# A hybrid attention block: a fourth split buffer, and q and k of three head groups transposed on TensorE

## The chip, the cores and the metric

The kernel runs on one core of a Trainium2 chip. The metric is device time in microseconds, the median of several executions. Engines are named as in the profile: PE is TensorE (PEld its weight loads), DVE is VectorE, ACT is ScalarE, POOL is GpSimd, SP is SyncE, which only issues transfers here.

## The reference

One transformer layer over 2048 tokens of width 1024, in float32:

```python
u = rms_norm(h, norm1_w)
dq, dk, dv, sq, sk, sv = split(u @ w_in)              # 512 columns each
# differential attention: 4 heads, two softmax maps each (QK norm, T5 bias, chunk-causal mask)
attn = softmax(q0 @ k0.T + bias) - lam * softmax(q1 @ k1.T + bias);  y_A = attn @ v
# stick-breaking attention: 8 heads of 64, strictly causal
z = q @ k.T / 8
rem = reverse exclusive cumsum over keys of log_sigmoid(-z)
y_B = exp(log_sigmoid(z) + rem) @ v
h = h + concat(norm(y_A), norm(y_B)) @ w_out
u2 = rms_norm(h, norm2_w)
h = h + (silu(u2 @ w_gate) * (u2 @ w_up)) @ w_down     # 2816 hidden columns
```

## The kernel before

float32 factors are split into two float16 parts, hi and lo, and every product is made of three float16 products. The work has eight head groups. Groups 0 to 3 hold one differential head each (two maps), groups 4 to 7 two stick-breaking heads each. After attention come the output projection, which starts beside the last group's attention, and the feed-forward, which does not use any of the code that the change touches.

**Projection of a group.** `proj` goes over 16 tiles of 128 tokens. `proj_tile` makes 24 matmuls of 384 columns into a PSUM tile `pj`. The pool `psj` has two of these. `proj_out` copies v, and for groups 4 to 7 q and k, out of PSUM as hi and lo parts (`split_psum`: the hi part on ScalarE or VectorE, the lo part on VectorE). q and k go into the tile `st`, of which there are two. After every fourth tile `proj_batch` makes the transposed operands of the scores: `kT` and the upper half of `qT` by DMA transposes from `st` (L381), and the lower half of `qT`, which holds the same with hi and lo halves of the partitions swapped, by two copies within SBUF (L383). All of them are issued by SyncE. A group has four batches. `st` is allocated with six blocks of columns; q uses blocks 0 and 1, k blocks 2 and 3. The output projection later takes tiles of the same tag for its residual rows (L763).

**Stick-breaking attention of a group.** A unit is one block of 128 queries, one head (m) and up to 1024 keys (b). `stage_a` does a unit: score matmuls into `sc` (L457, four PSUM buffers), two sigmoids on ScalarE (L563, L566), a product scan on VectorE (L568), a multiplication on VectorE or GpSimd (L569), and then `split_t`: the hi part by a cast on ScalarE (L89, by way of `to16`), the lo part by a subtraction on GpSimd (L98, by way of `tt`), both into a tile `s16`, of which there are SB, and a DMA transpose of it into one of five tiles `aT` (L412). `stage_b` multiplies `aT` with v on TensorE (L467). Five units lie between the two (PD).

**Order.** Each engine and SyncE's queue work in order. The order is made by the framework's planner from the program's order, priorities and its own estimate of durations. Projections of group g+1 are spread over the attention of group g by `advance`. Where a step may run on several engines, `pick` takes the engine with the lowest tally of estimated work.

The buffer counts and the split of probabilities:

```python
QB, KB, ZB, AB, SB, PD = 4, 7, 9, 5, 3, 5
s16 = s16p.tile([P, 2048], F16, tag="s16", bufs=SB, name=nm("s16"))
to16(s16[:, :n], src, n, he)
tt(s16[:, n : 2 * n], src, s16[:, :n], ALU.subtract, n, le)
SP.dma_start_transpose(aT[:, : 2 * n // P, :], s16[:, : 2 * n])
```

Of the kernel before, what the change touches and what calls it, by code (L numbers as in the profile page):

```python
# [11 lines left out]
F32 = mybir.dt.float32  # L12
F16 = mybir.dt.float16
# [8 lines left out]
S, D, P = 2048, 1024, 128  # L22
# [13 lines left out]
KW = {"A": 1.0, "D": 1.0, "P": 1.0}  # L36
AHEAD = 2
AHN = 0
QB, KB, ZB, AB, SB, PD = 4, 7, 9, 5, 3, 5
XL = (0, 4, 5, 2, 1, 6, 3)  # L40
CU = 3
WE = "AP"
# [17 lines left out]
def block(tc, a, out):  # L60
    nc = tc.nc
    PE, ACT, DVE, POOL, SP = nc.tensor, nc.scalar, nc.vector, nc.gpsimd, nc.sync
    top = ExitStack()
    with top:
# [8 lines left out]
        def note(e, ns):  # L73
            load[e] += ns * KW[e]

        def pick(**cost):
            e = min(cost, key=lambda k: load[k] + cost[k] * KW[k])
            load[e] += cost[e] * KW[e]
            return e
# [5 lines left out]
        def to16(dst, src, n, engines="ADP", psum=False):  # L85
            cost = {"A": 0.84 * n + 110, "D": (1.05 if psum else 0.53) * n + 70, "P": 1.1 * n + 80}
            e = pick(**{k: cost[k] for k in engines})
            if e == "A":
                ACT.copy(dst, src)  # L89
            elif e == "D":  # L90
                DVE.tensor_copy(dst, src)
            else:
                POOL.tensor_scalar(dst, src, 1.0, 0.0, op0=ALU.mult, op1=ALU.add)

        def tt(dst, a_, b_, op, n, engines="DP"):
            cost = {"D": 1.15 * n + 70, "P": 2.45 * n + 80}
            e = pick(**{k: cost[k] for k in engines})
            (DVE if e == "D" else POOL).tensor_tensor(dst, a_, b_, op)  # L98

        def pri(k):  # L100
            def deco(f):
                @functools.wraps(f)
                def g(*args):
                    with tc.high_priority(PRI[k]) if PRI[k] else nullcontext():
                        return f(*args)
                return g
            return deco

        def nm(s):
            uid[0] += 1  # L110
            return f"{s}{uid[0]}"
# [7 lines left out]
        id16 = cp.tile([P, P], F16, name="id16")  # L119
# [25 lines left out]
        def rstd(dst, ss, mul, eps):  # L145
            n = dst.shape[-1]
            if n > 1:
                ACT.activation(dst, ss, AF.Identity, bias=eps, scale=mul)
            else:
                DVE.tensor_scalar(dst, ss, mul, eps, op0=ALU.mult, op1=ALU.add)  # L150
            POOL.tensor_tensor(dst, dst, mhalf[:, :n], ALU.pow)
# [104 lines left out]
        psj = top.enter_context(tc.tile_pool(name="psj", bufs=2, space=PSUM, side="right"))  # L256
        pjs = ExitStack()
        pp = pjs.enter_context(tc.tile_pool(name="pp", bufs=2, side="right"))

        with ExitStack() as ph1:  # L260
# [95 lines left out]
            @pri("pb")  # L356
            def proj_batch(g, G, B):
                st, v, raw = B
                qT = sp.tile([P, 4, 4, P], F16, tag="qT", bufs=QB, name=nm("qT"))
                kT = sp.tile([P, 2, 4, P], F16, tag="kT", bufs=KB, name=nm("kT"))  # L360
                if g < 4:
                    rq = raw[:].rearrange("p t (c e) -> p t c e", e=64)
                    sq = st[:].rearrange("p c t s e -> p (c t s e)")[:, :2048].bitcast(F32)
                    ACT.activation(sq.rearrange("p (t c e) -> p t c e", t=4, c=4), rq, AF.Square)
                    note("A", 950)
                    ss = sm.tile([P, 16], F32, tag="ss", bufs=2, name=nm("ss"))
                    DVE.tensor_reduce(ss[:], sq.rearrange("p (c e) -> p c e", e=64), op=ALU.add, axis=AX.X)
                    rs = sm.tile([P, 16], F32, tag="rs", bufs=2, name=nm("rs"))
                    rstd(rs[:], ss[:], 2.0 ** -16 / 64, G["epsk"][:])
                    rsb = rs[:].rearrange("p (t c) -> p t c", c=4).unsqueeze(3).to_broadcast([P, 4, 4, 64])  # L370
                    DVE.tensor_tensor(rq, rq, rsb, ALU.mult)
                    note("D", 2300)
                    gb = gk[:].unsqueeze(1).unsqueeze(1).to_broadcast([P, 4, 2, 64])
                    tt(rq[:, :, 2:4, :], rq[:, :, 2:4, :], gb, ALU.mult, 512)
                    for o in range(2):
                        src = rq[:, :, 2 * o : 2 * o + 2, :]
                        d = st[:, 2 * o : 2 * o + 2].rearrange("p c t s e -> p t c s e")
                        to16(d[:, :, :, 0, :], src, 512)
                        tt(d[:, :, :, 1, :], src, d[:, :, :, 0, :], ALU.subtract, 512)
                for T, c in ((qT[:, 2:4], 0), (kT[:], 2)):  # L380
                    SP.dma_start_transpose(T.rearrange("p c t n -> p (c t) n"), st[:, c : c + 2].rearrange("p c t s e -> p (c t s e)"))  # L381
                for o in (0, 64):
                    SP.dma_start(qT[o : o + 64, 0:2].rearrange("p c t n -> p (c t n)"), qT[64 - o : 128 - o, 2:4].rearrange("p c t n -> p (c t n)"))  # L383
                G["q"].append(qT)
                G["k"].append(kT)
                G["v"].append(v)

            def proj(g, G, fresh=None):
                for t in range(NT):
                    if fresh is not None:  # L390
                        feed(t)
                        xt = ahead.pop(0)
                    else:
                        xt = pp.tile([P, 2 * D], F16, tag="xt", bufs=3, name=nm("xt"))
                        SP.dma_start(xt[:], xs[t])
                    if t % 4 == 0:
                        st = pp.tile([P, 6, 4, 2, 64], F16, tag="st", name=nm("st"))
                        v = sp.tile([P, 4, 256], F16, tag="v", bufs=KB, name=nm("v"))
                        raw = pp.tile([P, 4, 256], F32, tag="raw", name=nm("raw")) if g < 4 else None
                    pj = proj_tile(G, xt)  # L400
                    proj_out(g, G, pj, (st, v, raw), t % 4)
                    if t % 4 == 3:
                        proj_batch(g, G, (st, v, raw))
                    yield
# [223 lines left out]
            def feed(t):  # L628
                while nx[0] < min(NT, t + AHEAD + AHN):
                    nq.append(fresh(nx[0]))  # L630
                    nx[0] += 1
                while nx[1] < min(NT, t + AHEAD):
                    ahead.append(fresh_t(*nq.pop(0)))
                    nx[1] += 1
# [120 lines left out]
            def out_proj():  # L755
                for t in range(NT):
                    mt = pp.tile([P, 2 * D], F16, tag="xt", bufs=3, name=nm("mt"))[:].rearrange("p (k n) -> p k n", k=KT)
                    with tc.high_priority(PRI["wm"]) if PRI["wm"] else nullcontext():
                        mts.append(SP.dma_start(mt, ms[t]))
                    if t in spare:  # L760
                        xf = spare[t].bitcast(F32)
                    else:
                        xf = pp.tile([P, 6, 4, 2, 64], F16, tag="st", name=nm("xf"))[:].rearrange("p c t s e -> p (c t s e)").bitcast(F32)[:, :D]  # L763
                    SP.dma_start(xf, x[t * P : (t + 1) * P, :])
                    for h in range(2):
                        po = psj.tile([P, 512], F32, tag="pj", name=nm("po"))
                        for n in range(2):
                            q = 0
                            sl = slice(256 * n, 256 * n + 256)
                            for kt in range(KT):  # L770
                                for xi, wi in ((0, 0), (0, 1), (1, 0)):
                                    PE.matmul(po[:, sl], lhsT=mt[:, kt, P * xi : P * xi + P], rhs=wos[2 * h + n][wi][:, kt, :], start=q == 0, stop=q == 23)  # L772
                                    q += 1
                            xl = xf[:, 512 * h + 256 * n : 512 * h + 256 * n + 256]
                            DVE.scalar_tensor_tensor(xl, po[:, sl], kos[2 * h + n][:], xl, op0=ALU.mult, op1=ALU.add)  # L775
                    note("D", 1400)
                    SP.dma_start(hd[t], xf)
                    if t >= 12:
                        yield
                        continue  # L780
                    post(t, xf)
                    yield
# [459 lines left out]
```

## Time and profile before

| | |
|---|---|
| median of 3 executions | 2723.46 us (2717.96 to 2725.68) |
| the profiled execution | 2726.11 us, span 2724.3 us |
| granted TensorE clock, mean | 0.975 |
| busy: PE, DVE, ACT, POOL | 2471.4, 1945.7, 1345.8, 1569.3 us |
| HBM read and written | 265.27 MB, 151.52 MB |

Busy time is an average over stages. By the start times of the lines, groups 0 to 3 end near 600 us, groups 4 to 6 run to about 1120 us, group 7 with the output projection to about 1450 us, and the feed-forward from there to the end. In the profile, a row such as "ACT s L89 <- DMA aT<-s: 79.6, 57, 3.6" says that ScalarE stood idle before its instruction of line 89 that writes tile s, until a DMA of aT<-s landed: 79.6 us in total, 57 times, 3.6 us at most. "SPq" is the queue of SyncE; the time of a transfer there is the time its issue held the queue, and "to landing" runs from the start of the issue.

### The profile page before, as it was taken

The numbers are of one execution on the slowest core, as the hardware profiler recorded it, in microseconds if no ns is written. First come the engines' busy times: TensorE is split into PE (matmuls) and PEld (weight loads), VectorE is DVE, ScalarE is ACT, GpSimd is POOL, SyncE is SP. The second block draws the span as 40 slices with busy tenths as digits, with TensorE's granted clock in tenths as the row PEclk, the third lists the DMA queues.
The fourth block names the chain that finished last, engine by engine and source line by source line (L and its number), as shares of the span: only waits on it lengthen the run. The fifth ranks groups of instructions, "written<-read, shape, count | busy, mean of one in ns | idle before, by whom it ended". The sixth has DMA issues, their size and how long they took to land. (4 is left out here: it accounts for less than half of the span.)

```text
span 2724.3 us, 45559 instructions
## 1 busy us (share of the span) xinstructions
PE 2471.4 (91%) x17084; PEld 1404.6 (52%) x17084; DVE 1945.7 (71%) x3716; ACT 1345.8 (49%) x2483; POOL 1569.3 (58%) x1134
## 2 busy tenths in 40 slices
PE   7998989898888786779888999999999999999998
PEld 4655655555555453557775444444444444444443
DVE  6898979698888988876666877777786544444445
ACT  4665656567878878765644535444352112111121
POOL 2577767667767777765655666575674232323223
PEclk9999999999999997999999999999999999999999
DMA  6788797779999998996797675666749744545534
GB/s 223 205 168 176 149 195 161 177 170 206 208 207 203 205 183 159 205 202 199 203 268 266 237 245 201 220 215 212 251 170 350 279 175 145 224 151 190 208 125 166
DMA packets 649134, 551.92 MB, mean 203 GB/s; under 512 B 506624, under 2 KB 574208, under 8 KB 638672
## 3 DMA queue, kind: packets, MB, share of 16 engines
q1 hardware_dynamic: 647088, 546.92, 73.2%
q8 instruction: 134, 2.20, 0.3%
q0 software_dynamic: 512, 1.36, 0.2%
q10 hardware_dynamic: 1312, 0.72, 0.1%
q14 instruction: 88, 0.72, 0.1%
HBM read 265.27 MB, written 151.52 MB: 153 GB/s over the span
## 5 line engine op out<-in xcount | busy, mean ns | idle before, releaser
L329 PE MATMUL pj<-w,xt 128*128 128x384 f16 x3072 | 570.1, 333 | 26.3 <-DVE st L339 10.8
L98 POOL TENSOR_TENSOR s<-z,s 128x1024 f16<-128x1024 f32 (+7 forms) x288 | 477.5, 1667 | 99.3 <-ACT s L89 94.8
L329 PEld LDWEIGHTS <-xt 128*128 128x128 f16 x3072 | 298.5, 100 | 233.8 <-issue 38.2
L568 DVE TENSOR_TENSOR_SCAN z<-z,sc 128x512 f32<-128x512 f32 (+3 forms) x320 | 352.9, 1112 | 81.4 <-ACT sc L566 39.3
L1048 PE MATMUL pd<-wd,act 128*128 128x512 f16 x1848 | 405.3, 379 | 3.9 <-DVE hs L1054 2.4
L457 PE MATMUL sc<-kT,qT 128*128 128x512 f16 (+3 forms) x1280 | 339.6, 357 | 51.7 <-DVE z L568 16.2
L467 PE MATMUL yp<-v,aT 128*128 128x64 f16 (+1 forms) x4896 | 279.6, 207 | 91.5 <-DMA aT<-s 90.4
L467 PEld LDWEIGHTS <-aT 128*128 128x128 f16 x4896 | 242.2, 101 | 181.9 <-DMA aT<-s 120.2
L98 POOL TENSOR_TENSOR act<-cg,act 128x512 f16<-128x512 f32 x117 | 166.3, 1434 | 239.4 <-ACT act L1006 133.1
L950 PEld LDWEIGHTS <-wg 128*128 128x128 f16 x1848 | 181.1, 98 | 222.0 <-issue 7.9
L1048 PEld LDWEIGHTS <-act 128*128 128x128 f16 x1848 | 180.6, 98 | 222.7 <-issue 4.8
L950 PEld LDWEIGHTS <-wu 128*128 128x128 f16 x1848 | 181.9, 99 | 219.0 <-issue 6.5
L98 POOL TENSOR_TENSOR hs<-hs,cu 128x512 f32<-128x512 f32 x132 | 166.9, 1269 | 220.9 <-DVE hs L1054 76.0
L98 POOL TENSOR_TENSOR fst<-fst 128x512 f32<-128x512 f32 x97 | 182.6, 1883 | 161.3 <-DVE wd L224 89.9
L1054 DVE SCALAR_TENSOR_TENSOR hs<-pd,c,hs 128x512 f32<-128x512 f32 x192 | 141.6, 748 | 155.6 <-PE pd L1048 151.9
L89 ACT CAST s<-z 128x384 f16<-128x384 f32 (+7 forms) x216 | 171.6, 800 | 133.5 <-DMA aT<-s 104.5
L563 ACT ACTIVATE z<-sc,c 128x512 f32<-128x512 f32 (+3 forms) x320 | 207.0, 650 | 25.7 <-PE sc L457 18.5
L569 POOL TENSOR_TENSOR z<-z,z 128x512 f32<-128x512 f32 (+3 forms) x148 | 151.5, 1027 | 100.7 <-DVE z L568 85.6
L772 PE MATMUL po<-wo,mt 128*128 128x256 f16 x1536 | 180.1, 276 | 20.2 <-DVE xf L775 11.2
L1006 ACT CAST act<-cg 128x512 f16<-128x512 f32 x132 | 81.1, 616 | 218.1 <-DVE cg L1012 173.6
L950 PE MATMUL pm<-X,wg 128*128 128x512 f16 x792 | 179.7, 380 | 0.0
L950 PE MATMUL pm<-X,wu 128*128 128x512 f16 x792 | 179.4, 379 | 0.0
(237 smaller groups left out, 4139.3 us busy)
## 6 DMA issues: line engine op xcount, KB each, us to landing
xt<-xs SPq DMA_DIRECT2D x112, 512.0 KB, 4.2
hs<-hd SPq DMA_DIRECT2D x96, 512.0 KB, 4.4
hd<-hs SPq DMA_DIRECT2D x80, 512.0 KB, 4.4
split<-wg SPq DMA_DIRECT2D x11, 1792.0 KB, 11.3
split<-wu SPq DMA_DIRECT2D x11, 1792.0 KB, 10.4
split<-wd SPq DMA_DIRECT2D x11, 1792.0 KB, 10.5
wg<-split SPq DMA_DIRECT2D x11, 1792.0 KB, 7.2
wd<-split SPq DMA_DIRECT2D x11, 1792.0 KB, 8.9
```

The source lines that it names most:

```text
L89: ACT.copy(dst, src)
L98: (DVE if e == "D" else POOL).tensor_tensor(dst, a_, b_, op)
L329: PE.matmul(pj[:, :384], lhsT=xv[:, xi, kt, :], rhs=G["w"][:, wi, kt, :], start=n == 0, stop=n == 23)
L457: PE.matmul(sc[:, : 128 * w].rearrange("p (t n) -> p t n", n=P), lhsT=G["q"][i // 4][:, 2 - 2 * o + m, i % 4, :], rhs=G["k"][q][:, m, 0:w, ...
L467: PE.matmul(yp[:, y0 : y0 + wd], lhsT=aT[:, a_, :], rhs=v[:, v_ : v_ + wd], start=start and j == 0 and q == 0, stop=stop and j == nb - 1 a ...
L563: ACT.activation(om[:, lo:hi], sc[:, :w], AF.Sigmoid, scale=G["nkz"][:])
L568: DVE.tensor_tensor_scan(ov, ov, sc[:, :w], om[:, hi : hi + 1], op0=ALU.mult, op1=ALU.bypass)
L569: (DVE if e == "D" else POOL).tensor_tensor(be[:, lo:hi], beta, om[:, lo + 1 : hi + 1], ALU.mult)
L772: PE.matmul(po[:, sl], lhsT=mt[:, kt, P * xi : P * xi + P], rhs=wos[2 * h + n][wi][:, kt, :], start=q == 0, stop=q == 23)
L950: PE.matmul(ps_[:].rearrange("p (t n) -> p t n", n=P), lhsT=wv[:, wo, wi, 128 * kt : 128 * kt + 128], rhs=X[xo][:, :, xi, kt, :], start=st ...
L1048: PE.matmul(po[:], lhsT=act[:, ao, xi, 128 * j : 128 * j + 128], rhs=W["d"][:, wo, wi, :], start=start and u == 0 and q == 0, stop=u == nu ...
L1054: DVE.scalar_tensor_tensor(dst, po[:], kd[:], src, op0=ALU.mult, op1=ALU.add)
```

## The change

The count SB goes from 3 to 4. For groups 5, 6 and 7 `proj_batch` makes `kT` and both halves of `qT` on TensorE: eight transposes of 128x128 for k, eight for q, and sixteen of 64 columns for the swapped q, into three PSUM tiles of the pool `psj` read as 1024 float16. Each tile is copied to SBUF by ScalarE or VectorE (`to16` with the engines "AD"). Groups 0 to 4 keep the DMA transposes and copies. The tile `st` has four blocks in place of six.

```diff
-QB, KB, ZB, AB, SB, PD = 4, 7, 9, 5, 3, 5
+QB, KB, ZB, AB, SB, PD = 4, 7, 9, 5, 4, 5
...
-                for T, c in ((qT[:, 2:4], 0), (kT[:], 2)):
-                    SP.dma_start_transpose(T.rearrange("p c t n -> p (c t) n"), st[:, c : c + 2].rearrange("p c t s e -> p (c t s e)"))
-                for o in (0, 64):
-                    SP.dma_start(qT[o : o + 64, 0:2].rearrange("p c t n -> p (c t n)"), qT[64 - o : 128 - o, 2:4].rearrange("p c t n -> p (c t n)"))
+                if g > 4:
+                    for T, c, sw in ((kT[:], 2, 0), (qT[:, 2:4], 0, 0), (qT[:, 0:2], 0, 1)):
+                        pt = psj.tile([P, 512], F32, tag="pj", name=nm("qkt"))[:].bitcast(F16)
+                        for b in range(8):
+                            blk = st[:, c + b // 4, b % 4]
+                            if sw:
+                                for o in range(2):
+                                    PE.transpose(pt[64 * o : 64 * o + 64, P * b : P * b + P], blk[:, 1 - o, :], id16[:])
+                            else:
+                                PE.transpose(pt[:, P * b : P * b + P], blk.rearrange("p s e -> p (s e)"), id16[:])
+                        to16(T.rearrange("p c t n -> p (c t n)"), pt, 1024, "AD", True)
+                else:
...
-                        st = pp.tile([P, 6, 4, 2, 64], F16, tag="st", name=nm("st"))
+                        st = pp.tile([P, 4, 4, 2, 64], F16, tag="st", name=nm("st"))
...
-                        xf = pp.tile([P, 6, 4, 2, 64], F16, tag="st", name=nm("xf"))[:].rearrange("p c t s e -> p (c t s e)").bitcast(F32)[:, :D]
+                        xf = pp.tile([P, 4, 4, 2, 64], F16, tag="st", name=nm("xf"))[:].rearrange("p c t s e -> p (c t s e)").bitcast(F32)[:, :D]
```

More of the change, by code (lines that the diff above doesn't have):

```diff
@@ L379, in proj_batch @@
                         tt(d[:, :, :, 1, :], src, d[:, :, :, 0, :], ALU.subtract, 512)
-                for T, c in ((qT[:, 2:4], 0), (kT[:], 2)):
-                    SP.dma_start_transpose(T.rearrange("p c t n -> p (c t) n"), st[:, c : c + 2].rearrange("p c t s e -> p (c t s e)"))
-                for o in (0, 64):
-                    SP.dma_start(qT[o : o + 64, 0:2].rearrange("p c t n -> p (c t n)"), qT[64 - o : 128 - o, 2:4].rearrange("p c t n -> p (c t n)"))
+                if g > 4:
[10 more added lines that the diff above has]
+                else:
+                    for T, c in ((qT[:, 2:4], 0), (kT[:], 2)):
+                        SP.dma_start_transpose(T.rearrange("p c t n -> p (c t) n"), st[:, c : c + 2].rearrange("p c t s e -> p (c t s e)"))
+                    for o in (0, 64):
+                        SP.dma_start(qT[o : o + 64, 0:2].rearrange("p c t n -> p (c t n)"), qT[64 - o : 128 - o, 2:4].rearrange("p c t n -> p (c t n)"))
                 G["q"].append(qT)
```

## The prediction

> **What bounds the kernel now.** I read the page first, then the busy times by stage, then the waits of the slowest stage, then the queue of SyncE and single stretches of the timeline.
>
> ```profile
> span 2724.3 us, 45559 instructions
> core 0: us, PE busy (x) PEld busy (x) DVE busy (x) ACT busy (x) POOL busy (x), PEclk, DMA share, GB/s
> 120.00:600.00 480.00, 431.86 (x3442) 276.60 (x3440) 408.18 (x1217) 288.39 (x750) 337.93 (x240) 0.98 0.80 169
> 600.00:1210.00 610.00, 500.82 (x5177) 321.75 (x5176) 512.59 (x974) 477.68 (x887) 450.17 (x337) 0.94 1.00 198
> 1210.00:1450.00 240.00, 204.57 (x2131) 175.04 (x2129) 153.63 (x226) 122.22 (x191) 140.23 (x95) 0.97 0.82 238
> 1450.00:2724.00 1274.00, 1237.03 (x5789) 569.83 (x5786) 784.19 (x1091) 396.81 (x522) 592.22 (x407) 0.99 0.58 209
> 900.00:950.00 50.00, 38.05 (x420) 23.91 (x416) 45.34 (x64) 40.38 (x68) 40.06 (x26) 0.93 1.07 217
> ```
>
> The four long rows are differential attention, stick-breaking attention with the projections of the groups ahead, its end beside the output projection, and the feed-forward. The last is TensorE's (97% busy), and no line of the change runs in it. In 600 to 1210 no engine is full: VectorE 84%, TensorE 82%, ScalarE 78%, GpSimd 74%. The chain of waits on the page holds only the end of the feed-forward and says nothing here, so I go by the waits of this stage. Columns: who waited for whom, us in total, times, longest.
>
> ```profile
> ACT s L89 <- DMA aT<-s: 79.6, 57, 3.6
> POOL s L98 <- ACT s L89: 74.8, 58, 5.0
> PE yp L467 <- DMA aT<-s: 51.8, 45, 3.7
> DVE z L568 <- ACT sc L566: 34.3, 34, 2.3
> DVE z L568 <- ACT z L566: 30.8, 25, 3.9
> PE pj L329 <- DVE st L339: 9.1, 9, 1.8
> SPq L412 <- PE yp L467: 1.2, 1, 1.2
> ```
>
> ScalarE's cast L89 opens a split buffer (tag s16, three of them). It waits 57 times because the transfer that empties the buffer of three units ago has not landed. While it waits, the sigmoids behind it on ScalarE's queue are late, and VectorE's scan waits for these (34.3 + 30.8 us); GpSimd's subtraction waits too. The rate of a buffer follows from three rows of the same stage:
>
> ```profile
> L89 ACT CAST s<-z 128x1024 f16<-128x1024 f32 (+5 forms) x171 | 135.9, 801 | 84.0 <-DMA aT<-s 79.6 <-issue 1.7 <-POOL z L569 0.9
> L98 POOL TENSOR_TENSOR s<-z,s 128x1024 f16<-128x1024 f32 (+7 forms) x175 | 280.0, 1609 | 75.9 <-ACT s L89 74.8 <-POOL s L98 0.7
> L412 SPq DMA_TRANSPOSE aT<-s x175: 1167/1782/6477, 599.9 to 1209.0; - x175
> DMA to landing us min/median/max: 2.3/4.5/9.2
> ```
>
> A unit keeps its buffer for the cast (0.80), the subtraction (1.61) and 4.5 us from issue to landing: 6.9 us, plus waiting in the queues of GpSimd and SyncE. 171 units in 610 us are one each 3.57 us, so a slot comes round in 3 x 3.57 = 10.7 us. Only 3.8 us of a turn are left for the two queues, which is why the buffer runs out so often. By engine, a unit costs VectorE 512.6/171 = 3.00 us and ScalarE 2.79. So the three buffers, and behind them VectorE, set this stage.
>
> **The change part by part.** *Fourth buffer (SB).* It takes away ScalarE's 79.6 us of waits wherever the transfer is at most one unit late. The longest is 3.6 us, about one unit (3.57), so I expect nearly all to go. The shrunk st pays for it: two buffers of 6 x 4 x 2 x 64 fp16 become 4 x 4 x 2 x 64, 4096 bytes less per partition, what the new 2048 fp16 take. Columns 4 and 5 of st are read nowhere; cost nothing. What is late next: the scan itself, as VectorE is at 84%, and the subtraction on GpSimd. The five aT buffers are not next: SyncE waited for TensorE to free one once, 1.2 us.
>
> ScalarE's idle time in the stage is 610 - 477.7 = 132.3 us, of which this wait is 60%. VectorE waits 65.1 us for sigmoids. Taken in that proportion, 39 us of VectorE's waits go; the ends are 0 (something else is late) and 65.1.
>
> *Off SyncE's queue.* For three groups of four batches, 24 transposes (L381) and 24 copies (L383) go, and with them the wait of the copies for the q transpose. One batch in the timeline:
>
> ```profile
> 919.29 3.91 SPq L412 DMA_TRANSPOSE aT<-s  x2
> 923.29 1.59 SPq L381 DMA_TRANSPOSE qT<-st  x1
> 924.94 1.34 SPq L381 DMA_TRANSPOSE kT<-st  x1
> 928.61 1.11 SPq L383 DMA_DIRECT2D qT<-qT  x2
> 929.81 0.54 SPq L395 DMA_DIRECT2D xt<-xs  x1
> 930.45 2.32 SPq L412 DMA_TRANSPOSE aT<-s  x1
> ```
>
> ```profile
> L381 SPq DMA_TRANSPOSE qT<-st x12: 1231/1259/1595, 721.4 to 1200.9; - x12
> L381 SPq DMA_TRANSPOSE kT<-st x12: 1295/1335/2557, 725.2 to 1204.4; - x12
> L383 SPq DMA_DIRECT2D qT<-qT x22: 472/590/1054, 726.9 to 1167.0; - x22
>   PE sc L457: 0.9, 2
> ```
>
> The first three rows are the transfers between 720 and 1210 (two copies fall behind the window), the last is all that the scores waited for these transposes there. In the batch of the timeline, from 923.29 to 929.72 the queue is held, 6.4 us, 2.3 of it waiting. Behind stand the probabilities' transposes, whose buffers stay taken that long. Twelve batches hold it up to 77 us; with the issue times alone (two transposes near 1.3, two copies 0.6 each) 12 x 3.8 = 46 us. This shortens the same 10.7 us turn that the fourth buffer relieves, so I count no gain of its own: it is the reason why nearly all of ScalarE's waits go. SyncE's queue order changes only by what leaves it. The scores, which waited 0.9 us for q and k, are not late now and hide a later arrival of some microseconds.
>
> *TensorE's transposes.* 8 for k, 8 for q, 16 of half width for the swapped q: 32 a batch, 384 in all. An fp16 transpose is not in this trace. The nearest rows:
>
> ```profile
> 1238.91 0.74 PE L605 MATMUL xtr<-id,z 128*128 128x128 f32 x5
> 1256.21 0.49 PE L605 MATMUL xtr<-id,z 128*128 128x128 f32 x3
> 812.10 0.43 PE L467 MATMUL yp<-v,aT 128*128 128x64 f16 x9
> 813.16 0.69 PE L467 MATMUL yp<-v,aT 128*128 128x64 f16 x18
> L459 PE MATMUL sc<-tri,idb 128*128 128x128 bf16 x128 | 29.3, 230 | 0.0
> ```
>
> Two more fp32 transposes in a run took 0.25 us more, 0.125 each. Nine more fp16 matmuls of 64 columns took 0.26 more, 0.029 each. A lone 16-bit matmul of 128 columns took 0.230. So the bounds are 0.029 and 0.230, 11 to 88 us in all. I take twice the fp16 step, as the moving identity has 128 columns: 0.06, 23 us. TensorE has 610 - 500.8 = 109 us idle in the stage; that covers it, so it costs nothing. Without the cover it costs its 23 us.
>
> The Trainium skill ("TensorE: Matmul & The Clock Gate", Part 4: PE-mode transpose) gives about 275 ns for a 128x128 transpose inside a kernel and says that such work does not raise the clock. By that, 384 would take an estimated 106 us, all of the idle time; the runs of three and five above, near 0.15 us a transpose in fp32, speak against it.
>
> *Evictions.* Each of the 36 PSUM tiles (1024 fp16) is copied out by ScalarE or VectorE, whichever the kernel's tally has lower.
>
> ```profile
> L338 DVE TENSOR_SCALAR v<-pj 128x128 f16<-128x128 f32 x46 | 12.7, 277 | 5.5 <-PE pj L329 5.0 <-PE yp L467 0.4
> L338 DVE TENSOR_SCALAR st<-pj 128x256 f16<-128x256 f32 x19 | 7.9, 414 | 0.0
> L793 ACT COPY z<-xtr 128x512 f32<-128x512 f32 x24 | 13.9, 591 | 31.5 <-PE xtr L605 31.5
> L89 ACT CAST x<-z 128x1024 f16<-128x1024 f32 x16 | 16.8, 1063 | 9.5 <-DVE z L98 4.6 <-POOL z L98 3.0 <-DMA aT<-s 1.4
> ```
>
> VectorE: 277 + 896 x (414 - 277)/128 = 1236 ns, an estimate. ScalarE: near 1063. Half each is 18 x 1.24 = 22 us on VectorE and 19 on ScalarE (end: all on VectorE, 44). VectorE is the engine next in line, so 84% of its 22 is charged, 19 us. The copies also queue behind scans (mean 1.1 us), and until they are done the two pj buffers hold back the projection.
>
> *The fourth buffer elsewhere.* In 1210 to 1450 the same cast waits:
>
> ```profile
> ACT s L89 <- DMA xcd<-x: 12.0, 6, 4.8
> ACT s L89 <- DMA aT<-s: 8.4, 3, 6.0
> ```
>
> Together 20.4 us, where TensorE is 85% busy and ScalarE 51%. I take 4 us, ends 0 and 20. Before 600, in 120 to 600, it waits little, and ScalarE is 60% busy; nothing is counted:
>
> ```profile
> ACT s L89 <- DMA aT<-s: 16.5, 5, 5.3
> ```
>
>
> *Sum.* By waits: 39 + 4 - 19 = 24 us gained. By work: VectorE then has 512.6 + 22 = 535 us in the stage; its best 50 us above (45.34) is 91% with these waits still in it, so at 92% the stage takes 581 us, 29 less, with the tail 33. I take 29, between the two. The profiled execution took 2726.1 us (span 2724.3); that gives 2697. It stands 2.7 us above the median of the three runs, 2723.5, so the forecast for the median is 2694 us.
>
> **The rivals.** *The wait is handed on (same).* VectorE has 535 us to do; at 88% this is 608 us, and nothing is gained. For it: differential attention runs VectorE at 85%, no higher, with a fifth of these waits (16.5 us), GpSimd keeps 74% and TensorE its clock of 0.94. Against: those 65.1 us of VectorE waits name ScalarE, and ScalarE's name the buffer. Time: 2718 to 2724.
>
> *TensorE stalls (slower).* Place: the 36 tiles in the two pj buffers, shared with the projection, in order on TensorE's queue; the swapped tile needs the k tile copied out. At a lone 0.230 us, 10.7 transposes are 2.5 us a tile, and if each then waits as the longest pj wait above (1.8), a tile costs 4.3 us. TensorE would have 500.8 + 36 x 4.3 = 656 us in a stage of 610: 46 longer, the tail gives 4 back, 2766. It decides from (610 - 500.8)/36 = 3.0 us a tile. For it: the planner has a new order to make, and waits on pj exist. Against: other matmuls stand between, and rows in runs are far below 0.230. By the figure of the Trainium skill above ("TensorE: Matmul & The Clock Gate", Part 4), the transposes alone would be an estimated 2.9 us a tile, just short of that point.
>
> *All of it (much faster).* The 65 us of waits go, evictions fall into what remains idle, the tail's 20 follow: 85 us, 2639.
>
> **How the numbers follow.** My forecast, a gain between 9 and 60 us: 0.59. Much faster: 0.12. Handed on: 0.14. TensorE stalls: 0.15. About 0.3%, 8 us, is what a measurement can tell from no change. Faster is therefore 0.71 (both fast cases), same 0.14, slower 0.15. The range goes from 2650, most of the way to the 85 us, to 2724, no gain; the stall lies outside. The likeliest case alone is 2663 to 2715.
>
> **What would show it.** Right: ScalarE's waits for the aT transfers under 25 us in the stage, VectorE's waits for sigmoids under 35, its share above 90%, the first output-projection matmuls some 25 us earlier, no q or k transfer after the fifth group, 384 transposes with a step near 0.06 us and copies near 1.1 us, the feed-forward unchanged. Wrong: projection matmuls or transposes waiting for a pj copy for over 30 us, a mean transpose step above 0.2 us, the granted clock below 0.94, or the scan waiting as long as before with another name behind it.

## The result and the profile after

The changed kernel takes 2734.6 us (median of 5), the kernel before 2725.6 us beside it: a ratio of 1.0036, 95% interval 1.0024 to 1.0049. It is slower by 0.36%, a little more than the 0.3% that the prediction took as the least that can be told from no change; a gain of 29 us had been forecast. The profiled execution has a span of 2731.3 us, 7.0 above that of before.

Busy time by stage, in the columns used before:

```profile
120.00:600.00 480.00, 426.58 (x3373) 272.88 (x3371) 402.41 (x1205) 286.99 (x738) 337.89 (x239) 0.97 0.78 166
600.00:1210.00 610.00, 510.22 (x5480) 331.36 (x5480) 517.60 (x976) 489.64 (x909) 452.92 (x343) 0.94 0.91 184
1210.00:1450.00 240.00, 210.86 (x2209) 180.55 (x2210) 170.38 (x242) 126.33 (x199) 137.07 (x95) 0.99 0.79 225
```

These windows are fixed in time while the work slides through them, so I take milestones too. The rows of the scan tell when stick-breaking attention begins and ends (start of the first and of the last of 320). First the row of before, then that of the changed kernel:

```profile
L568 DVE TENSOR_TENSOR_SCAN z<-z,sc x320: 453/1270/1281, 613.5 to 1379.7; 128x512 f32<-128x512 f32 x88, 128x128 f32<-128x128 f32 x24, 128x256 f32<-128x256 f32 x24, 128x384 f32<-128x384 f32 x24
```

```profile
L580 DVE TENSOR_TENSOR_SCAN z<-z,sc x320: 454/1271/1282, 619.9 to 1388.0; 128x512 f32<-128x512 f32 x88, 128x128 f32<-128x128 f32 x24, 128x256 f32<-128x256 f32 x24, 128x384 f32<-128x384 f32 x24
```

6.4 of the 7.0 us are lost before the first scan, in differential attention, where the change does nothing but give a fourth buffer and a smaller st. From the first to the last scan it is 768.1 us after 766.2: no gain in the stage that the change was aimed at. The rest of the span, after the last scan, is 1.3 us shorter. The waits of the stage, 600 to 1210, of the changed kernel:

```profile
POOL z L581 <- DVE z L580: 83.1, 57, 6.2
PE yp L479 <- DMA aT<-s: 51.7, 39, 4.2
DVE z L580 <- ACT sc L578: 33.4, 27, 4.1
POOL s L98 <- ACT s L89: 32.0, 26, 3.4
ACT z L575 <- PE sc L471: 17.9, 13, 3.6
ACT z L575 <- PE sc L469: 17.5, 17, 2.9
DVE z L580 <- ACT z L578: 16.1, 23, 2.9
ACT s L89 <- POOL z L581: 13.7, 10, 2.4
ACT s L89 <- DMA aT<-s: 12.9, 12, 2.4
PE pj L329 <- DVE st L339: 8.9, 3, 4.9
```

The wait that the fourth buffer was to remove is nearly gone: 12.9 us for 79.6. But VectorE's waits for sigmoids went only from 65.1 to 49.5. ScalarE now waits longer for scores (35.4 us, before 19.6) and for the multiplication on GpSimd (13.7, before 0.9), and GpSimd's wait for the scan rose from 66.3 to 83.1. The rows of before, in the same stage:

```profile
POOL z L569 <- DVE z L568: 66.3, 50, 4.3
ACT z L563 <- PE sc L457: 17.1, 14, 2.9
ACT z L563 <- PE sc L459: 2.5, 2, 2.3
ACT s L89 <- POOL z L569: 0.9, 1, 0.9
```

The output projection, which was to begin some 25 us earlier, begins 30 us later. Its first matmul, first before and then in the changed kernel, starts at 1191.4 and 1221.3 us:

```profile
L772 PE MATMUL po<-wo,mt x1536: 269/273/421, 1191.4 to 1453.0; 128*128 128x256 f16 x192
L784 PE MATMUL po<-wo,mt x1536: 269/273/421, 1221.3 to 1460.8; 128*128 128x256 f16 x192
```

The transposes themselves, 384 in twelve batches, with the copies that empty their tiles, and one run of them on the timeline (start, duration):

```profile
L389 PE MATMUL qkt<-id,st x192: 219/219/314, 726.6 to 1216.7; 128*128 128x128 f16 x192
L387 PE MATMUL qkt<-id,st x192: 216/219/316, 733.6 to 1218.2; 128*64 128x128 f16 x192
L89 ACT COPY qT<-qkt x12: 1012/1057/1114, 732.3 to 1219.8; 128x1024 f16<-128x1024 f16 x12
L91 DVE COPY qT<-qkt x12: 681/691/694, 734.7 to 1217.0; 128x1024 f16<-128x1024 f16 x12
L89 ACT COPY kT<-qkt x9: 1012/1038/1077, 776.5 to 1216.5; 128x1024 f16<-128x1024 f16 x9
L91 DVE COPY kT<-qkt x3: 665/667/693, 731.1 to 1056.0; 128x1024 f16<-128x1024 f16 x3
```

```profile
730.01 0.90 PE L389 MATMUL qkt<-id,st 128*128 128x128 f16 x13 [0.50 <-DVE st L339]
```

Thirteen in a run take 0.90 us; each after the first adds (0.90 - 0.22)/12 = 0.057 us.

### The profile page after: what moved, and what is told of

Same layout as the page of the kernel before. It is cut to its first block, busy times and chain, and to the rows that moved or that the text cites. A ratio compares the mean times of both kernels' runs of the same rounds, so it can differ in the third digit from the quotient of the medians.

```text
span 2731.3 us, 46286 instructions
## 1 busy us (share of the span) xinstructions
PE 2481.9 (91%) x17468; PEld 1420.3 (52%) x17468; DVE 1963.6 (72%) x3726; ACT 1363.3 (50%) x2501; POOL 1574.2 (58%) x1142
## 5 line engine op out<-in xcount | busy, mean ns | idle before, releaser
L329 PE MATMUL pj<-w,xt 128*128 128x384 f16 x3072 | 575.9, 335 | 28.9 <-DVE st L339 8.9
L581 POOL TENSOR_TENSOR z<-z,z 128x512 f32<-128x512 f32 (+2 forms) x155 | 159.8, 1034 | 136.7 <-DVE z L580 119.3
L784 PE MATMUL po<-wo,mt 128*128 128x256 f16 x1536 | 176.9, 274 | 10.7 <-DVE wo L787 3.7
L504 DVE TENSOR_SCALAR_CACHE_REDUCE z<-sc,c 128x512 f32<-128x512 f32 (+3 forms) x256 | 160.6, 648 | 27.5 <-PE sc L469 24.3
```

The lines of the kernel that those rows point to most:

```text
L329: PE.matmul(pj[:, :384], lhsT=xv[:, xi, kt, :], rhs=G["w"][:, wi, kt, :], start=n == 0, stop=n == 23)
L504: DVE.tensor_scalar(z[:, lo : lo + f], sc[:, :f], kz_d[:], None, op0=ALU.mult, op1=ALU.max, accum_out=mx[:, m, nx : nx + 1])
L581: (DVE if e == "D" else POOL).tensor_tensor(be[:, lo:hi], beta, om[:, lo + 1 : hi + 1], ALU.mult)
```

## The experiments

After the result there were these theories. A: the split buffer did not set the pace, and its waits are handed on in the same loop. B: the buffer helps and the TensorE transposes lose it. C: the planner's new order moves the time by as much as the change does. Ratios are to the kernel before, run on the same chip.

### The two halves, and two kernels with another order of the same work

The fourth buffer alone:

```diff
-QB, KB, ZB, AB, SB, PD = 4, 7, 9, 5, 3, 5
+QB, KB, ZB, AB, SB, PD = 4, 7, 9, 5, 4, 5
...
-st = pp.tile([P, 6, 4, 2, 64], ...)      # in proj and in out_proj
+st = pp.tile([P, 4, 4, 2, 64], ...)
```

> The fourth split buffer alone (with the smaller st), all transposes by DMA. Theory A (the buffer was not what set the pace: its waits are handed to other places in the same loop): ScalarE's cast waits fall from 79.6 us to under 25 us in 600 to 1210, and the time stays within 8 us of before, 2718 to 2734. Theory B (the buffer helps, the TensorE transposes lose it again): 2690 to 2710, faster by 15 to 35 us. Theory C (the planner's new order moves the time by as much as the change does): anywhere from 2715 to 2740.

Measured: 2730.9 us, 1.0023 (1.0013 to 1.0032). The time is as theory A had it, but the cast waits are 33.1 us, not under 25. Its waits in the stage, 600 to 1210:

```profile
ACT s L89 <- DMA aT<-s: 33.1, 26, 5.4
DVE z L568 <- ACT sc L566: 32.6, 31, 3.5
DVE z L568 <- ACT z L566: 12.9, 15, 3.5
```

The transposes alone (`if g > 4:` and its block, SB = 3, st with six blocks):

> The TensorE transposes of the last three groups alone, three split buffers as before. Theory A: no cost and no gain beyond SyncE's freed queue, 2715 to 2730. Theory B (the tiles in the two pj buffers delay the projections): 2740 to 2765, slower by 15 us or more, with projection matmuls waiting longer for pj. Theory C: 2715 to 2740.

Measured: 2730.4 us, 1.0015 (1.0005 to 1.0025).

The kernels before and after with

```diff
-                        note("A", 1.7 * w + 400)
+                        note("A", 1.7 * w + 410)
```

> The kernel before with one constant of the tally changed (410 for 400 in the note of ScalarE's work in stage_a), which does the same work in another planned order, a few copies on the other engine. Theories A and B, in which the order is not the cause: within 4 us of before, 2721 to 2730. Theory C: it moves by 5 to 15 us, either way.

Measured: 2730.4 us, 1.0021 (1.0012 to 1.0030).

> The changed kernel with the same constant changed (410 for 400). Theories A and B: within 4 us of the changed kernel, 2730 to 2739. Theory C: it moves by 5 to 15 us from the changed kernel, either way.

Measured: 2729.9 us, 1.0012 (1.0003 to 1.0022), 0.24% under the changed kernel.

Theory B falls: neither half gains, neither loses 15 us. A new order of the very same work moves the time up in one kernel and down in the other, by 6 and 7 us by the ratios and by 4 and 5 us by the medians, as much as either half does. That is about theory C's lower bound of 5, so a difference of 0.2% between two such kernels says nothing about a mechanism, and part of the changed kernel's 0.36% can be its order. In the run with the transposes alone ScalarE waits nearly as long as before the change, so SyncE's freed queue did not by itself shorten the turn of the buffer as I had thought. Its stage, 600 to 1210:

```profile
ACT s L89 <- DMA aT<-s: 76.9, 52, 4.3
DVE z L580 <- ACT sc L578: 30.4, 33, 4.5
DVE z L580 <- ACT z L578: 29.0, 26, 4.7
```

With the fourth buffer 33.1 us of these waits are left while SyncE still makes q and k, 12.9 and 27.4 in the two kernels in which it does not. Neither of the steps from 79.6 to 33.1 and on to 12.9 shortened the stage: first to last scan is 766.2 us before, 767.9 with the buffer alone and 768.1 in the changed kernel.

### What sets the pace instead: ablations of the changed kernel

Each leaves out part of the computation of one engine or queue. Each is planned anew, so its gain carries the 0.2% of a new order. Half of the scan:

```diff
-DVE.tensor_tensor_scan(ov, ov, sc[:, :w], ...)
+DVE.tensor_tensor_scan(ov[:, : w // 2], ov[:, : w // 2], sc[:, : w // 2], ...)
```

> The changed kernel with the scan of stick-breaking attention over half of its columns (the other half of the cumulative product is left out): about 150 us less for VectorE between 600 and 1400. Theory A1 (VectorE is what the fourth buffer hands the pace to): 2600 to 2660, the largest gain of these four runs. Theory A2 (TensorE and its order set the pace): 2710 to 2735. Theory A3 (no engine alone; a loop of short waits through all of them): 2680 to 2715.

Measured: 2702.7 us, 0.9915 (0.9883 to 0.9947).

One product of three in the projection of groups 4 to 7:

```diff
-for xi, wi in ((0, 0), (0, 1), (1, 0)):
+for xi, wi in ((0, 0),) if "kz" in G else ((0, 0), (0, 1), (1, 0)):
...      # and the last matmul of the eight, not of 24, closes the sum
```

> The changed kernel with one product in place of three in the projection of groups 4 to 7 (the two products with low parts are left out): two thirds of TensorE's projection work of those groups, some 170 us of its busy time between 540 and 1200, go. Theory A1: 2710 to 2735. Theory A2: 2600 to 2660, the largest gain. Theory A3: 2680 to 2715.

Measured: 2714.6 us, 0.9957 (0.9937 to 0.9977).

Half of each transpose of the probabilities, the hi half alone:

```diff
-SP.dma_start_transpose(aT[:, : 2 * n // P, :], s16[:, : 2 * n])
+k = n if le == "P" else 2 * n
+SP.dma_start_transpose(aT[:, : k // P, :], s16[:, :k])
...      # and the product with v reads the hi half in place of the lo half
```

> The changed kernel with only the high half of the stick-breaking probabilities transposed by DMA (the low half is computed and left out of the product, which reads the high half twice): half of the bytes of these transposes go, the work of all engines stays. Theories A1 and A2: 2720 to 2735. Theory A3: 2700 to 2720. A fourth, that the DMA queues set the pace: 2640 to 2690.

Measured: 2703.9 us, 0.9915 (0.9886 to 0.9944).

The same, without the subtraction on GpSimd (`if le != "P":` ahead of the `tt`):

> As the run before, and GpSimd's subtraction for the stick-breaking groups left out too: some 280 us less for GpSimd between 600 and 1210, and the split buffer is held 1.6 us less and waits for no GpSimd. Theories A1 and A2: within 10 us of the run with half of the transposes. Theory A3: another 20 to 50 us faster than that run. If GpSimd set the pace: over 60 us faster.

Measured: 2643.7 us, 0.9694 (0.9666 to 0.9722).

Busy time of the four in 600 to 1210, in the order of the runs:

```profile
600.00:1210.00 610.00, 516.99 (x5601) 337.93 (x5602) 408.99 (x992) 498.19 (x926) 458.21 (x349) 0.94 0.92 188
```

```profile
600.00:1210.00 610.00, 421.99 (x4682) 274.31 (x4680) 523.79 (x988) 497.97 (x921) 460.37 (x351) 0.84 0.90 183
```

```profile
600.00:1210.00 610.00, 519.07 (x5693) 340.62 (x5694) 534.31 (x1004) 501.49 (x928) 463.64 (x353) 0.94 0.62 139
```

```profile
600.00:1210.00 610.00, 550.70 (x6194) 380.89 (x6195) 508.84 (x967) 496.62 (x909) 361.89 (x336) 0.98 0.69 154
```

In the first three, VectorE falls to 67% busy, TensorE to 69%, the DMA engines to 62%, and each time the kernel gains only 0.8 to 1.2% on the changed one (1.0036 less 0.9915, 0.9957 and 0.9915). None of the three alone is the engine or queue whose time the stage takes. The last ablation gained 60.2 us, 2.2%, on top of the third: more than the 20 to 50 us of theory A3, and at the 60 us that were to speak for GpSimd. It is not GpSimd alone that it relieves: with the subtraction out of the tally, the multiplications moved from VectorE to GpSimd. Its row, then that of the changed kernel, both in 600 to 1210:

```profile
L583 POOL TENSOR_TENSOR z<-z,z 128x512 f32<-128x512 f32 (+3 forms) x275 | 279.9, 1023 | 215.2 <-DVE z L582 170.6 <-DVE z L568 30.9 <-DVE m L195 7.5
```

```profile
L581 POOL TENSOR_TENSOR z<-z,z 128x512 f32<-128x512 f32 (+2 forms) x131 | 132.1, 1012 | 93.0 <-DVE z L580 83.1 <-DVE z L568 5.5 <-DVE z L566 3.7
```

So it shortens the way from the cast to the transfer and lightens two engines at once. Which of these is the larger part stays open, and with it how much of the pace is GpSimd's.

Then three ablations in one kernel, after the single ones were known:

> The changed kernel with three of the ablations together: half of the scan, one product of three in the projection of groups 4 to 7, and half of the probabilities' transposes left out (each alone gained 20 to 32 us on the changed kernel, 2734.6). Theory H (several limits side by side, each as long as the others, so that taking one away leaves the rest): together far more than the 83 us of the sum, 2560 to 2630. Theory I (one chain through all engines, in which each gives its own part): the sum, 2640 to 2660. Theory J (a limit that none of the three touches, ScalarE or GpSimd, is close behind): less than the sum, 2670 to 2700.

Measured: 2644.8 us, 0.9702 (0.9678 to 0.9725), 3.3% under the changed kernel. The single gains make 1.21 + 0.79 + 1.21 = 3.2%. They add, as theory I has it: a chain that goes through several engines and queues in turn, to which each gives a part. If the limits lay side by side, the three together would have gained far more than their sum. From the first to the last scan nearly the same holds: 768.1 us in the changed kernel, 743.9, 740.7 and 740.1 with one ablation (24.2 + 27.4 + 28.0 = 79.6 less), and with all three 682.1 (86.0 less):

```profile
L581 DVE TENSOR_TENSOR_SCAN z<-z,sc x320: 322/736/749, 625.4 to 1307.5; 128x256 f32<-128x256 f32 x88, 128x64 f32<-128x64 f32 x24, 128x128 f32<-128x128 f32 x24, 128x192 f32<-128x192 f32 x24
```

Gains would also add if each limit held alone in a stretch of its own. The starts of the scans speak against that: from the 41st to the 81st scan the changed kernel takes 88.4 us, and 79.3, 75.0 and 79.1 with one ablation, so all three gain in the same stretch. The links of the chain themselves are argued from the waits, not shown, and ScalarE's part was not tried.

### Where GpSimd's multiplications go

```diff
-e = pick(D=1.04 * w + 155, P=2.4 * w + 100)
+e = pick(D=1.04 * w + 155)
```

> The changed kernel with every multiplication of stick-breaking attention on VectorE, none on GpSimd: GpSimd loses some 150 us of work and its waits for the scan (119 us in the whole trace), VectorE gains some 90 us of work. Theory G (GpSimd's queue, in which the subtraction stands behind a multiplication that waits for a scan, holds the split buffers and sets the pace): 2690 to 2715. Theory A1 (VectorE sets it): 2750 to 2800, slower.

Measured: 2754.4 us, 1.0107 (1.0081 to 1.0132). The gain of theory G does not come: freed of the waits for scans, GpSimd waits for ScalarE's casts instead (210.5 us), and first to last scan takes 787.1 us, 19 more. The edit also gives VectorE 21.6 us more to do in the stage (539.2 after 517.6), so it does not show GpSimd's queue to cost nothing; it shows that this exchange is a loss.

```profile
600.00:1210.00 610.00, 503.28 (x5264) 322.79 (x5265) 539.18 (x982) 496.29 (x941) 311.17 (x202) 0.92 0.86 175
POOL s L98 <- ACT s L89: 210.5, 92, 6.4
```

### How much a split buffer is worth: two of them

```diff
-QB, KB, ZB, AB, SB, PD = 4, 7, 9, 5, 3, 5
+QB, KB, ZB, AB, SB, PD = 4, 7, 9, 5, 2, 5
```

> The kernel before with two split buffers in place of three. A slot then has to come round in 2 x 3.57 = 7.1 us to keep the pace, and a unit holds it 6.9 us without any queueing. If three buffers are the knee of the curve (so that a fourth had nothing to give): slower by 60 to 200 us, 2785 to 2925, with ScalarE's waits for the buffer above 150 us. If the buffer is a small part of the chain at any count: slower by 5 to 30 us, 2731 to 2756.

Measured: 2840.6 us, 1.0423 (1.0397 to 1.0449). From two buffers to three the kernel gains 4.2%, from three to four (the fourth alone) it loses 0.2%, no more than a new order does. So three are the knee for the time of the whole kernel. ScalarE's wait in the whole run with two, then with three:

```profile
ACT s L89 <- DMA aT<-s: 183.6, 102, 6.2
```

```profile
ACT s L89 <- DMA aT<-s: 104.5, 65, 6.0
```

The wait has the same name and differs by less than a factor of two. With two buffers, a third is worth 115 us; with three, the changed kernel took most of what is left away in the stage, without a gain. Not all of the 115 us need be the buffer's: with two, first to last scan takes 95 us longer (861.2 after 766.2), the first scan comes 13.5 us later, and the granted clock in 600 to 1210 was 0.83 in place of 0.94.

### Other uses of the 4 KB

The fourth buffer for the stick-breaking groups only:

```diff
-QB, KB, ZB, AB, SB, PD = 4, 7, 9, 5, 4, 5
+QB, KB, ZB, AB, SB, PD = 4, 7, 9, 5, 3, 5
+sbn[0] += he == "A"
+fourth = he == "A" and sbn[0] % 4 == 0
-s16 = s16p.tile([P, 2048], F16, tag="s16", bufs=SB, ...)
+s16 = s16p.tile([P, 2048], F16, tag="s16b" if fourth else "s16", bufs=1 if fourth else SB, ...)
```

> The changed kernel with the fourth split buffer for the stick-breaking groups alone (every fourth unit takes a buffer of its own tag; differential attention keeps three). Theory D (the fourth buffer slows differential attention by some 5 to 11 us and gains little after it): the first stick-breaking transfers come as early as in the kernel before, and the time is 2720 to 2730, 5 to 12 us under the changed kernel. Theory C (order alone): 2725 to 2740, with no link to the stage.

Measured: 2718.2 us, 0.9971 (0.9958 to 0.9984), 16 us under the changed kernel, a little more than theory D had. With the tally constant at 410:

> The changed kernel with the fourth split buffer for the stick-breaking groups alone (2718.2), with the tally constant 410 for 400. Theory D (three buffers in differential attention are worth their 11 us whatever the order): 2712 to 2725. Theory C (a lucky order): 2726 to 2736.

Measured: 2721.9 us, 0.9992 (0.9980 to 1.0004).

The first scan starts at 611.5 and 613.9 us in these, as with three buffers everywhere (613.5 in the kernel before, 614.3 with the transposes alone, 611.6 in the reordered kernel before, 615.3 with the sixth aT buffer below). With four buffers in all groups it starts at 619.9, 618.7 and 618.8 (changed kernel, fourth buffer alone, reordered changed kernel). So the 5 to 6 us before the first scan belong to the fourth buffer in differential attention. They appear in each of the kernels that have it, and go when it goes. The ones that have it share one planned order in that part, so whether another order with four buffers would lose it too was not tried.

The stage itself is shorter too in these two kernels: 756.9 and 759.2 us from the first to the last scan, after 766.2 before, 768.6 with the transposes and three buffers, and 768.1 and 764.8 in the changed kernel and its reordered copy.

```profile
L584 DVE TENSOR_TENSOR_SCAN z<-z,sc x320: 453/1270/1282, 611.5 to 1368.4; 128x512 f32<-128x512 f32 x88, 128x128 f32<-128x128 f32 x24, 128x256 f32<-128x256 f32 x24, 128x384 f32<-128x384 f32 x24
L584 DVE TENSOR_TENSOR_SCAN z<-z,sc x320: 452/1270/1282, 613.9 to 1373.1; 128x512 f32<-128x512 f32 x88, 128x128 f32<-128x128 f32 x24, 128x256 f32<-128x256 f32 x24, 128x384 f32<-128x384 f32 x24
```

So a fourth buffer beside the transposes can gain 7 to 9 us in the stage, a quarter to a third of the forecast. The units have four buffers here as in the changed kernel, where this gain is missing; why it is missing there was not tried.

A tenth z4 buffer (the tag of the float32 tiles in SBUF that hold, among others, a unit's sigmoids and products), and a sixth aT buffer, both with three split buffers, DMA transposes and the smaller st:

```diff
-QB, KB, ZB, AB, SB, PD = 4, 7, 9, 5, 3, 5
+QB, KB, ZB, AB, SB, PD = 4, 7, 10, 5, 3, 5     # first kernel
+QB, KB, ZB, AB, SB, PD = 4, 7, 9, 6, 3, 6      # second kernel
```

> The kernel before with the smaller st, and the memory spent on a tenth score buffer (tag z4) in place of a fourth split buffer. Theory E (a unit needs two z4 buffers, and they are the next to run out): 2695 to 2715. Theory C or a loop in which a buffer count is not the limit: 2722 to 2734.

Measured: 2715.7 us, 0.9965 (0.9951 to 0.9980), just past the upper end of theory E's range.

> The kernel before with the smaller st, the memory spent on a sixth aT buffer, and the product with v six units behind the scores in place of five. Theory F (TensorE stands in its queue for a transfer that has not landed, 52 us in the stage before and after the change, and this passes on to the scores): 2690 to 2715, with TensorE's waits for aT under 25 us. Otherwise 2720 to 2735.

Measured: 2726.8 us, 1.0007 (0.9994 to 1.0021). With a sixth aT buffer TensorE waits as long for aT in the stage as before (51.8 us). So the edit did not remove the wait of theory F, and whether that wait passes on to the scores stays untested.

```profile
PE yp L467 <- DMA aT<-s: 52.9, 51, 5.8
```

The gain of the tenth z4 buffer lies before the stage: the first scan starts at 602.5 us, 11.0 earlier, and first to last is 764.8 us. It was meant for the stick-breaking units. Put together with the transposes, with SB = 3:

> The changed kernel with three split buffers and a tenth z4 buffer: the TensorE transposes with the memory spent on z4. If the 12 us of the tenth z4 buffer (won before the stick-breaking groups) are independent of the transposes, whose own price was 0 to 5 us: 2712 to 2722. If they exclude each other: 2725 to 2735.

Measured: 2710.0 us, 0.9940 (0.9921 to 0.9958), faster than both kernels.

> The kernel with TensorE transposes, three split buffers and ten z4 buffers (2710.0), with the tally constant 410 for 400. If its gain is that of the tenth z4 buffer and not of one order: 2703 to 2718. If it is a lucky order: 2720 to 2730.

Measured: 2704.2 us, 0.9924 (0.9909 to 0.9938). Its scans:

```profile
L580 DVE TENSOR_TENSOR_SCAN z<-z,sc x320: 454/1271/1282, 603.5 to 1356.1; 128x512 f32<-128x512 f32 x88, 128x128 f32<-128x128 f32 x24, 128x256 f32<-128x256 f32 x24, 128x384 f32<-128x384 f32 x24
```

Here the stage too is shorter, 752.6 us after 766.2. With ten z4 buffers the transposes gain some 10 us there (764.8 to 754.7 and 752.6), with nine and three split buffers they gained nothing (768.6). A new order alone moved this stretch by 3 to 5 us (766.2 to 770.7, 768.1 to 764.8). Why the transposes gain with the tenth buffer was not tried.

Both buffers at once, paid by kT and v (`4, 6, 10, 5, 3, 5` and the tag of its own):

> The changed kernel with a tenth z4 buffer and the fourth split buffer for the stick-breaking groups alone; kT and v have six buffers in place of seven to make room. If the two gains (12 us before 670, some 7 us after) add: 2702 to 2712. If the shorter kT and v hold up the projection: 2715 to 2735.

Measured: 2717.1 us, 0.9969 (0.9953 to 0.9985). The first scan comes late (621.9 us, where ten z4 buffers alone had 602.5), and the stage is the shortest of all complete kernels, 743.9 us. The shorter kT and v would explain the first, which was not shown. The second speaks for a stage that answers to buffers when two kinds are added together, but it is one order, and work that was done before the late start may be missing from the stage.

## Why the prediction was wrong, point by point

- **The failed step** is in the part on the fourth buffer: of VectorE's 65.1 us of waits for sigmoids, 39 were to go, in proportion to ScalarE's idle time. The cause was removed as forecast (79.6 to 12.9 us, under the 25 named), but only 15.6 us of VectorE's waits went, and the time from first to last scan did not fall (768.1 us after 766.2). ScalarE's idle time in the stage is 610 - 489.6 = 120 us after 132, though its longest wait is 67 us shorter; its work there grew by the same 12 us, in which 20 us of copies of q and k are contained. It waits nearly as long as before, under other names. The proportion took a sum of waits for a share of the path.
- **The second leg of the sum**, VectorE at 92%, was an upper bound on the gain that I used as a forecast. VectorE reached 517.6/610 = 85%. With a fifth of its work in the stage left out, the kernel gained 1.2%: it was not next in line. "So the three buffers, and behind them VectorE, set this stage" holds, for the buffers, for the step from two to three (4.2%) and not from three to four; VectorE was not shown to set the stage in either. That a slot's 10.7 us exceed the 6.9 us of its unit by only 3.8 showed that the buffer is often full; it did not show that the units would come faster.
- **Outside the stage** I counted nothing before 600 and 4 us gained after 1210. Before the first scan 6.4 us were lost, and that is nearly all of the measured slowdown in the profiled executions. After the last scan 1.3 us were gained.
- **The order.** "SyncE's queue order changes only by what leaves it" does not hold: the planner makes a new order. With four buffers in both, from the first batch on TensorE the loads of xt stand at other places among the probabilities' transposes, the output projection begins 30 us later than before, and one constant of the tally moves the time by 0.2%. The sum had no term for it.
- **TensorE's transposes** were right: 16.4 + 8.3 = 24.7 us of busy time forecast as 23, a step of 0.057 us forecast as 0.06. The rival in which they stall at the pj buffers did not happen: projection matmuls wait 8.9 us for VectorE's copies (9.1 before). The Trainium skill's 275 ns a transpose ("TensorE: Matmul & The Clock Gate", Part 4: PE-mode transpose) is not the step that these runs show in a train of them; the duration recorded for a single one, 219 ns, is below it too.
- **The copies** were cheaper on VectorE: 15 of 36 went there at 0.69 us, where 1.24 was worked out from fp32 rows; ScalarE's 1.05 us was forecast as 1.06. The Trainium skill ("VectorE: DVE Perf Modes", Why PSUM operands drop a tier) allows a 16-bit source in PSUM twice the rate of fp32, and the 0.69 us agrees: the fp32 rows give 137 ns for 128 columns more and 140 ns besides, and 1024 columns at half of that rate make 0.55 + 0.14 us. The 19 us charged were too much by about half.
- **SyncE's queue.** The 46 to 77 us that it no longer gives to q and k shortened nothing by themselves: with three buffers the casts still waited 76.9 us. That they are a reason why nearly all of ScalarE's waits go is borne out in part: 33.1 us are left with the fourth buffer alone, 12.9 and 27.4 with both.
- **The rival that came closest** was the wait handed on: the stage kept its pace, as that rival had it, but the wait went to no single engine, and its 88% on VectorE was not the reason (VectorE stood at 85%). Its 2718 to 2724 us lie below the 2734.6 measured. The slower side had been given a mechanism that did not occur, so that the time came out slower at all was luck for that side.

## What to carry to other kernels

A sum of waits at one place, on an engine that is itself 78% busy, is no gain to be had: ask what the next instruction on that engine would wait for, and prove it by leaving work out. If three ablations gain little each and their gains add up, that speaks for one chain through in-order queues rather than for limits side by side, and one more buffer at one link may only move the wait to the next link. Where a planner makes the order, time the same work in another order before believing a difference of 0.2%, and look at the stages that the edit was not meant for.

## What was not expected of the hardware

When TensorE had less to do, it ran at a lower clock: with two of the projection's three products left out (69% busy in the stage) the granted clock fell to 0.84, from 0.94 in the changed kernel. The same score matmul of 512 columns took 437 ns in the mean there, after 396, so the ablation gave back part of what it saved. The rows of the changed kernel, then of the ablation, in 600 to 1210:

```profile
L469 PE MATMUL sc<-kT,qT 128*128 128x512 f16 x406 | 125.4, 396 | 21.6 <-DVE z L580 6.0 <-DVE z L568 5.6 <-DVE z L581 5.4
L469 PE MATMUL sc<-kT,qT 128*128 128x512 f16 x408 | 139.5, 437 | 45.5 <-DVE z L580 20.2 <-DVE z L568 10.3 <-DVE z L566 7.7
```

The Trainium skill ("TensorE: Matmul & The Clock Gate", Part 1: The HAM clock gate) says that idle stretches throttle the array, and these clocks agree. VectorE copies 1024 fp16 from PSUM in 0.69 us, ScalarE in 1.05.
